# A bidirectional hybrid encoder layer on one Trainium2 core: which queue begins the decay rows' loads

## Chip, cores, metric

One Trainium2 chip, one of its NeuronCores. A core has five engines that run on their own and wait for one another through semaphores: TensorE (PE: matmuls, and PEld, its weight loads), VectorE (DVE), ScalarE (ACT), GpSimd (POOL) and SyncE (SP). Transfers between HBM and SBUF are begun by an instruction in the queue of SyncE, ScalarE or GpSimd and are then carried out by 16 DMA engines. Each queue is worked off in order: an instruction that waits for a semaphore holds back everything behind it in that queue.

The metric is the device time of one execution in microseconds, as the median of several runs.

## The reference

One layer, batch 1, 2048 tokens of width 1024. A normed and modulated input is multiplied by one large matrix; its columns feed two branches, neighbourhood attention on a grid of 64 columns and a bidirectional mLSTM with 4 heads of 128. The outputs are concatenated, multiplied by an output matrix and added to the input through a gate.

```python
mod = c_act @ w_ada + b_ada; shift, scale, gate = split(mod, 3)
h = rmsnorm(x, norm_w) * (1 + scale) + shift
proj = h @ w_in + b_in
na_out = neighbourhood_attention(na_q, na_k, na_v, rpb) * silu(na_z)
h_fwd, h_bwd = mlstm_chunkwise(mq, mk, mv, i_f, f_f), flip(mlstm_chunkwise(flip(...)))
ml_out = norm((h_fwd + h_bwd) * sigmoid(ml_o)) * ml_norm_w * silu(ml_z)
x = rmsnorm(x + gate * (concat(na_out, ml_out) @ w_out), final_norm_w)
```

The part that matters here lies in the mLSTM. Inside a chunk, the score of position t against position s is weighted by a decay matrix:

```python
Dlog = where(lower, b[..., :, None] - b[..., None, :] + i_pre[..., None, :], -inf)
S = einsum('bhntd,bhnsd->bhnts', q, k) * exp(Dlog - m_t[..., None])
```

The reference takes chunks of 64; the kernel takes chunks of 128 (CH), of which there are 16 for each head and direction. With g = i - b and m the running maximum that stabilises the exponent, the weight is exp(g[s] - m[t]) under the triangular mask.

## The kernel before

All matrices are float32 and are multiplied in three passes of float32r parts (high x high, high x low, low x high), so each product of a weight block with a token tile is 24 matmuls.

The kernel runs in stages. `phase1` prepares h, then computes the projection block by block, 256 columns each. `tok_blocks` (blocks 2 to 5) has token-major outputs: `vo_group` for the mLSTM's v and output gate (blocks 2 and 3; blocks 0 and 1 were done in `start`), `nav_group` for the attention's v (blocks 4 and 5). A block has 4 groups of 4 token tiles. PE writes a tile into one of four PSUM banks (`pp`), VectorE adds the bias row and writes it into one of two staging tiles (`stvo`, `stv`; L495 and L460), and a store issued by SyncE brings a full staging tile to HBM (`d_ck<-stvo` at L502, `d_vna<-stv` at L464). The store of a group is put into a list by `defer` and written out at the `flush` at the end of the following group; the group after that needs the same staging tile again. `conv_blocks` (blocks 6 to 9) computes the mLSTM's k and q with channel-major outputs (`pc`), which ScalarE takes from PSUM (`u`, L769). Then `phase1b` runs the mLSTM with the remaining projections as filling, and `phase2` the attention and the output projection, the latter in an order written out by hand.

Beside the matmuls of `tok_blocks` runs `self.chain`, a generator of small steps; each token tile advances it by one. It first computes the gates' prefix sums (`gate_chain`), which ends with writing -m for all 128 rows (direction, head, chunk) to HBM as `d_mneg` (L666), and then the decay matrices (`decays`). These are 16 tiles `dec` of 128 x 1024, one for each head and group of four chunks, each with both directions:

- load: two transfers (L698), one for each direction; four rows of `d_mneg`, 512 numbers in all, are read and written into all 128 partitions (256 KB each). There are two buffers (`wgate` and `gacc`), so the load for tile n+2 needs the store of tile n to have landed;
- GpSimd adds the mask (L706);
- ScalarE takes eight exponentials, one for each chunk and direction (L710);
- ScalarE's queue stores the two halves into `d_ck` (L712), where the mLSTM reads them later.

Between these steps `gate_row` sums the gate's weights, with VectorE multiplying loaded tiles `wide` (L397, L404, L406; loaded by SyncE), and SyncE also issues the weight blocks (`raw`, L189), the bias rows (`brow`, L467) and the bias tables (`d_t<-d_e`, L547). ScalarE rounds a weight block to its high part (L191) and GpSimd subtracts for the low part (L192); GpSimd also sets a column of ones in each `stvo` tile (L484). ScalarE applies the sigmoid of the output gate (L499).

Outside `phase2` the order of each engine's queue is made by the framework's scheduler when the program is built: it takes the instructions of the source, with their dependences, and places them, so that a queue need not follow the source's order exactly.

Of the kernel before, what the change touches and what calls it, by code (L numbers as in the profile page):

```python
# [15 lines left out]
P = 128  # L16
# [42 lines left out]
class Kernel:  # L59
# [621 lines left out]
    def decays(self, pool, beside):  # L681

        nc = self.nc
        mask = pool.tile([P, 2, CH], F32, name="mask")
        nc.gpsimd.memset(mask, 0.0)
        nc.gpsimd.affine_select(out=mask[:, 0, :], in_=mask[:, 0, :], pattern=[[1, CH]], compare_op=ALU.is_ge, fill=-BIG, base=0, channel_multiplier=-1)
        nc.gpsimd.affine_select(out=mask[:, 1, :], in_=mask[:, 1, :], pattern=[[-1, CH]], compare_op=ALU.is_ge, fill=-BIG, base=0, channel_multiplier=1)
        groups = [(h, gi) for h in range(MH) for gi in range(NG)]
        tiles = {}

        def load(n):
            h, gi = groups[n]
            flat = pool.tile([P, D], F32, tag=("wgate", "gacc")[n % 2], bufs=1, name=f"dec_{h}_{gi}")
            t = flat.rearrange("p (d c t) -> p d c t", d=2, c=4)
            for d in range(2):
                r = d * 64 + h * NC + 4 * gi
                src = self.d_mneg[r : r + 4].rearrange("r t -> (r t)").unsqueeze(0)
                nc.sync.dma_start(flat[:, d * 512 : (d + 1) * 512], src.broadcast_to([P, 512]))  # L698
            tiles[n] = t

        load(0)
        load(1)
        yield
        for n, (h, gi) in enumerate(groups):
            t = tiles.pop(n)
            nc.gpsimd.tensor_tensor(t, t, mask.unsqueeze(2).broadcast_to([P, 2, 4, CH]), ALU.add)  # L706
            for d in range(2):
                for o in range(4):
                    c = 4 * gi + o
                    nc.scalar.activation(t[:, d, o, :], t[:, d, o, :], AF.Exp, bias=self.cols["g"][:, d, h, c : c + 1])  # L710
                dst = self.d_ck[h, 4 * gi : 4 * gi + 4, :, 641 + d * CH : 641 + (d + 1) * CH].rearrange("c p t -> p c t")
                nc.scalar.dma_start(dst, t[:, d])  # L712
            yield
            next(beside, None)
            yield
            if n + 2 < len(groups):
                load(n + 2)
            yield
        for _ in beside:
            pass  # L720
# [905 lines left out]
```

## Time and profile before

| | us |
|---|---|
| median of 3 runs | 1402.96 (1400.93 to 1407.99) |
| span of the profiled execution | 1394.1 |
| PE busy in the span | 1312.1 |
| ScalarE, VectorE, GpSimd busy | 527.9, 828.9, 294.3 |

The page of the profiled execution gives its span, from the first to the last instruction; what lies around it in a run's time is not shown by itself. A row of the waits reads: engine and line, what it waited for, us in total, number of times, longest. A row of the timeline reads: start in us, duration, engine, line, operation, out<-in, count, and in brackets the idle time before it with what ended it. "SPq" is SyncE's queue, "ACTq" and "POOLq" those of ScalarE and GpSimd; L numbers are lines of the kernel. Neighbouring instructions of the same line are merged (x4), and the duration then covers all of them with the gaps between.

What the DMA queues carried over the whole run (packets, MB, share of 16 engines' span; q1 is begun by SyncE, q10 by ScalarE, q0 by GpSimd):

```
q1 hardware_dynamic: 178062, 186.45, 49.8%
q0 software_dynamic: 21504, 37.73, 11.1%
q10 hardware_dynamic: 70024, 38.02, 9.6%
```

GpSimd begins no transfer before the mLSTM is over: its first one in the trace of before starts at 998.5 us.

### The profile page before, as it was taken

What the parts mean: (1) busy time and instruction counts of PE and PEld (TensorE: products, weight loads), DVE (VectorE), ACT (ScalarE), POOL (GpSimd) and SP (SyncE); (2) the same over time, 40 slices, a digit from 0 to 9 for tenths busy, and PEclk for the clock granted to TensorE, in tenths of its full rate; (3) what the DMA queues carried; (4) which work ended last, traced back from release to release, by engine and by line L of the source; (5) the groups of instructions that cost most, each with busy time, mean ns of one, the idle gap of its engine ahead of it and who ended that gap; (6) DMA issues with size and microseconds to landing.
All of it is one profiled execution on the core that took longest, in us unless ns stands there. A gap on an engine that the chain in (4) does not pass through costs nothing.

```text
span 1394.1 us, 23365 instructions
## 1 busy us (share of the span) xinstructions
PE 1312.1 (94%) x8052; PEld 1124.8 (81%) x8052; DVE 828.9 (59%) x2563; ACT 527.9 (38%) x1129; POOL 294.3 (21%) x321
## 2 busy tenths in 40 slices
PE   2989999898999999999999998999998999999996
PEld 2989998898877787788878877788886888888885
DVE  6583323111355569146767877877646787777674
ACT  4642335423232323113323322333335555555551
POOL 4453212424101010001213002212312211112111
PEclk9999999999999999999999999999999999999998
DMA  9799438677558675554676787856597897876862
GB/s 325 218 288 222 121 100 236 176 197 193 142 111 213 146 188 159 170 160 140 190 212 200 235 236 216 223 144 182 170 270 220 185 227 166 198 191 168 190 162 74
DMA packets 269707, 263.67 MB, mean 189 GB/s; under 512 B 33466, under 2 KB 230074, under 8 KB 269590
## 3 DMA queue, kind: packets, MB, share of 16 engines
q1 hardware_dynamic: 178062, 186.45, 49.8%
q0 software_dynamic: 21504, 37.73, 11.1%
q10 hardware_dynamic: 70024, 38.02, 9.6%
q8 instruction: 64, 1.05, 0.3%
q14 instruction: 53, 0.43, 0.1%
HBM read 177.57 MB, written 92.72 MB: 194 GB/s over the span
## 4 chain that ended last, share of the span: by engine, by line
PE 53%; DMA 6%; DVE 3%; issue 2%; ACT 1%; POOL 1%; POOLq 0%; SPq 0%; ACTq 0%; DVEq 0%
PE pq L861 21%; PE y L1416 11%; PE pO L1379 4%; PE pT L1364 4%; DMA kv<-d_ck 2%; PE pi L1089 2%; PE pc L425 2%; PE pc L426 2%; PE pc L427 2%; PE px L1087 2%; PE pS L1336 1%; PE pS L1337 1%; PE dc L1035 1%; DMA tab<-d_t 1%; PE a L1074 1%
## 5 line engine op out<-in xcount | busy, mean ns | idle before, releaser
L861 PE MATMUL pq<-hhi,whi_a 128*128 128x512 f32 x512 | 210.7, 412 | 0.8 <-ACT u L769 0.8
L861 PE MATMUL pq<-hlo,whi_a 128*128 128x512 f32 x512 | 210.5, 411 | 0.0
L861 PE MATMUL pq<-hhi,wlo_a 128*128 128x512 f32 x512 | 210.4, 411 | 0.0
L1343 ACT ACTIVATE pbuf<-pbuf,mn 128x480 f32<-128x480 f32 (+5 forms) x128 | 76.4, 597 | 105.3 <-DVE mn L1342 105.3
L861 PEld LDWEIGHTS pq<-hhi,whi_a 128*128 128x128 f32 x512 | 97.6, 191 | 19.2 <-ACT u L769 1.2
L861 PEld LDWEIGHTS pq<-hhi,wlo_a 128*128 128x128 f32 x512 | 97.6, 191 | 18.0
L861 PEld LDWEIGHTS pq<-hlo,whi_a 128*128 128x128 f32 x512 | 97.6, 191 | 17.9
L1416 PE MATMUL y<-hhi,whi_a 128*128 128x512 f32 x256 | 86.0, 405 | 3.4 <-ACT hhi L1317 2.8
L1416 PE MATMUL y<-hhi,wlo_a 128*128 128x512 f32 x256 | 84.3, 399 | 0.0
L835 POOL TENSOR_TENSOR wlo_a<-rawq,whi_a 128x1024 fp32r<-128x1024 f32 x20 | 48.3, 2414 | 166.2 <-ACT whi_a L834 126.9
L1111 POOL TENSOR_TENSOR hm<-hm,ck 128x128 f32<-128x128 f32 x64 | 26.5, 414 | 264.8 <-DVE hm L1110 178.8
L1342 DVE CUSTOM_DVE_ANT_0 pbuf<-pS,tab 128x480 f32<-128x480 f32 (+5 forms) x128 | 64.8, 540 | 28.3 <-PE pS L1337 21.3
L425 PE MATMUL pvo<-whi_b,hhi 128*128 128x256 f32 x256 | 74.7, 292 | 7.1 <-DVE stvo L495 7.1
L1092 ACT ACTIVATE num<-px,gtile 128x129 f32<-128x129 f32 x120 | 38.3, 365 | 97.4 <-PE px L1087 77.4
L1019 DVE TENSOR_SCALAR wv<-kv,gtile 128x129 f32<-128x129 f32 x120 | 36.9, 314 | 63.9 <-PE dc L1035 32.2
L427 PE MATMUL pvo<-whi_b,hlo 128*128 128x256 f32 x256 | 73.5, 287 | 0.0
L426 PE MATMUL pvo<-wlo_b,hhi 128*128 128x256 f32 x256 | 73.5, 287 | 0.0
L710 ACT ACTIVATE dec<-dec,gtile 128x128 f32<-128x128 f32 x128 | 42.0, 392 | 71.6 <-POOL dec L706 60.8
L495 DVE TENSOR_TENSOR stvo<-pvo,brow 128x256 f32<-128x256 f32 x64 | 26.4, 419 | 71.2 <-PE pvo L427 54.9
L460 DVE TENSOR_TENSOR stv<-pv,brow 128x256 f32<-128x256 f32 x32 | 12.4, 420 | 87.9 <-DMA d_vna<-stv 48.4
L1379 PE MATMUL pO<-pt,v 128*64 128x128 f32 (+3 forms) x832 | 61.3, 282 | 0.3 <-ACT pt L1366 0.3
L1364 PE MATMUL pT<-ident,pbuf 128*128 128x128 f32 (+2 forms) x416 | 59.1, 280 | 0.0
(298 smaller groups left out, 3575.2 us busy)
## 6 DMA issues: line engine op xcount, KB each, us to landing
ck<-d_ck SPq DMA_DIRECT2D x64, 384.5 KB
kv<-d_ck SPq DMA_DIRECT2D x120, 128.5 KB
rawq<-in_w_main_dram SPq DMA_DIRECT2D x28, 512.0 KB
raw<-in_w_main_dram SPq DMA_DIRECT2D x20, 512.0 KB
d_ck<-stvo SPq DMA_DIRECT2D x16, 514.0 KB
x<-in_x_dram SPq DMA_DIRECT2D x16, 512.0 KB
wada<-in_w_ada_dram SPq DMA_DIRECT2D x32, 256.0 KB
dec<-d_mneg SPq DMA_DIRECT2D x32, 256.0 KB
```

The source lines that it names most:

```text
L425: nc.tensor.matmul(ps, lhi(k), rhi(k), start=(k == 0), stop=False)
L426: nc.tensor.matmul(ps, lhi(k), rlo(k), start=False, stop=False)
L427: nc.tensor.matmul(ps, llo(k), rhi(k), start=False, stop=(k == KT - 1))
L710: nc.scalar.activation(t[:, d, o, :], t[:, d, o, :], AF.Exp, bias=self.cols["g"][:, d, h, c : c + 1])
L835: nc.gpsimd.tensor_tensor(lo[:, :, cs], raw, hi[:, :, cs].bitcast(F32), ALU.subtract)
L861: nc.tensor.matmul(patch_ps(ps) if patch else ps, w, self.htok(h, g, k, patch), start=(k == 0 and n == 0), stop=(k == KT - 1 and n == 2))
L1092: nc.scalar.activation(num[:, d, :], px[:, d, :], AF.Copy, scale=self.cols["inter"][:, d, h, c : c + 1])
L1342: nc.vector.tensor_tensor_reduce(pt[:, :nk], ps, tabs[place[u]][j][:, :nk], 1.0, 3e38, ALU.add, ALU.min, mn)
L1343: nc.scalar.activation(pt[:, :nk], pt[:, :nk], AF.Exp, bias=mn, scale=-1.0, accum_out=sums[:, j : j + 1])
L1364: nc.tensor.transpose(ps[:cs, i, :], pts[j][:, i * cs : (i + 1) * cs], self.ident)
L1379: nc.tensor.matmul(po[j * HD : (j + 1) * HD, :], v[:n, h * HD : (h + 1) * HD], pt[j][:n, i, :], start=(i == 0), stop=(i == nch - 1))
L1416: nc.tensor.matmul(y, m[:, k, :], w[k][:, cs], start=(k == 4 and n == 0), stop=(k == 3 and n == 2))
```

## The change

The two loads of a `dec` tile are begun by GpSimd's queue. Source, destination, size, number and place in the source stay as they are, and so do all other transfers.

```diff
@@ in decays(), load(n)
             for d in range(2):
                 r = d * 64 + h * NC + 4 * gi
                 src = self.d_mneg[r : r + 4].rearrange("r t -> (r t)").unsqueeze(0)
-                nc.sync.dma_start(flat[:, d * 512 : (d + 1) * 512], src.broadcast_to([P, 512]))
+                nc.gpsimd.dma_start(flat[:, d * 512 : (d + 1) * 512], src.broadcast_to([P, 512]))
             tiles[n] = t
```

## The prediction

> **What bounds the kernel now.** I read the waits of the whole run first, to see which engine sets the end. TensorE is busy 94% of the span, so only a stretch in which it stands still can pay for anything.
>
> ```profile
> PE 1312.1 (94%) x8052; PEld 1124.8 (81%) x8052; DVE 828.9 (59%) x2563; ACT 527.9 (38%) x1129; POOL 294.3 (21%) x321
> ```
>
> The 32 loads are issued between 195.8 and 340 us, in the token-major blocks. The windows table of that stage (PE busy, PEld, DVE, ACT, POOL, then granted clock, DMA share, GB/s) and the waits of PE in it:
>
> ```profile
> 190.00:230.00 40.00, 40.00 (x340) 40.00 (x339) 11.98 (x20) 17.87 (x31) 12.51 (x7) 1.00 0.72 190
> 230.00:270.00 40.00, 32.90 (x261) 32.28 (x260) 11.84 (x17) 17.22 (x38) 9.72 (x6) 0.96 0.72 195
> 270.00:310.00 40.00, 39.11 (x324) 37.90 (x323) 5.73 (x14) 14.33 (x35) 12.47 (x6) 1.00 0.77 189
> 310.00:345.00 35.00, 32.12 (x264) 30.91 (x262) 3.60 (x9) 12.37 (x34) 15.10 (x7) 1.00 0.75 180
> 345.00:360.00 15.00, 11.98 (x87) 11.98 (x88) 2.69 (x7) 5.37 (x17) 3.33 (x2) 0.78 0.88 244
> ...
> PE pvo L425 <- DVE stvo L495: 7.1, 3, 3.7
> PE pv L425 <- DVE stv L460: 6.8, 2, 5.9
> ```
>
> PE idles 7.1 + 0.9 + 2.9 + 3.0 = 13.9 us here, which is the 7.1 + 6.8 of the two waits: always for VectorE to empty a PSUM bank. Behind each idle stretch the granted clock falls as well. Five-microsecond windows:
>
> ```profile
> 250.00:255.00 5.00, 3.32 (x18) 3.32 (x19) 2.62 (x5) 4.10 (x10) 0.32 (x2) 0.76 0.55 158
> ...
> 345.00:350.00 5.00, 1.98 (x9) 1.98 (x10) 1.42 (x4) 3.78 (x12) 3.33 (x2) 0.50 0.98 334
> 350.00:355.00 5.00, 5.00 (x38) 5.00 (x38) 0.42 (x1) 1.44 (x5) 0.00 (x0) 0.85 1.10 246
> ```
>
> Busy time by missing clock: 3.32 x 0.24 = 0.8 us after the earlier stops, 1.98 x 0.50 + 5 x 0.15 = 1.7 us after the last. So 13.9 + 2.5 = 16.4 us (1.2%) is the most that any change to this stage can win.
>
> Why is VectorE late? Its own wait rows, and what SyncE's queue waited for in the same stage:
>
> ```profile
> DVE stv L460 <- DMA d_vna<-stv: 48.4, 5, 16.1
> DVE gsum L406 <- DMA wide<-in_w_ada_dram: 24.0, 6, 10.2
> ...
> SPq L698 <- DMA d_ck<-dec: 65.7, 18, 9.0
> ```
>
> VectorE waits for stores and loads that SyncE issues, and SyncE stands 65.7 us in front of the decay loads (L698), each of which may only start when the store of the tile that held its buffer has landed. SyncE takes its instructions in order, so a store whose data is ready waits there too. The worst case, in SyncE's and VectorE's timelines:
>
> ```profile
> 326.05 0.24 SPq L417 DMA_DIRECT2D d_gate<-wide  x1
> 335.92 4.91 SPq L698 DMA_DIRECT2D dec<-d_mneg  x4
> 340.93 0.38 SPq L464 DMA_DIRECT2D d_vna<-stv  x1
> ...
> 319.38 0.42 DVE L460 TENSOR_TENSOR stv<-pv,brow 128x256 f32<-128x256 f32 x1 [2.42 <-PE pv L427]
> ...
> 347.54 1.42 DVE L460 TENSOR_TENSOR stv<-pv,brow 128x256 f32<-128x256 f32 x4 [16.14 <-DMA d_vna<-stv]
> ```
>
> The staging tile was full at 319.8; its store went out at 340.93, behind four decay loads, and VectorE got the tile back at 347.5. That is PE's 5.9 us stop.
>
> **The change, part by part.** Removed from SyncE: 32 issues and their waits. Added to GpSimd: the same 32 issues and waits, ahead of or between the mask additions (L706), the weight splits (L192) and the memsets (L484). Bytes and destinations stay.
>
> *The last stop.* With L698 gone, the store follows the 326.05 issue and can start about 14.6 us earlier (340.93 against 326.3), and VectorE with it, at 333. PE runs ahead of VectorE by four PSUM banks; a tile is 24 matmuls of 40/340 us, 2.8 us, so the lead is 11.3 us and 14.6 us removes the 5.9 us stop. With its clock: **-7.6 us**. Bounds: 0 (another transfer holds the store) to -7.6.
>
> *The stop of 0.9 us at 293.* The same pattern, with the pair of loads and then the store:
>
> ```profile
> 286.47 0.81 SPq L698 DMA_DIRECT2D dec<-d_mneg  x2
> 287.38 0.38 SPq L464 DMA_DIRECT2D d_vna<-stv  x1
> ```
>
> PE missed 0.9 us in this window, as much as the pair's issue alone kept the store back (286.47 to 287.38). Without it: **-0.9 us**, bounds 0 and -0.9.
>
> *The three stops between 230 and 251 us (7.1 us, 0.8 of clock)* hang on the gate row's weight loads:
>
> ```profile
> 223.08 1.52 SPq L698 DMA_DIRECT2D dec<-d_mneg  x2
> 226.32 0.33 SPq L397 DMA_DIRECT2D wide<-in_w_ada_dram  x1
> ...
> 240.73 1.61 SPq L698 DMA_DIRECT2D dec<-d_mneg  x2
> 242.44 0.37 SPq L397 DMA_DIRECT2D wide<-in_w_ada_dram  x1
> ```
>
> Without the decay loads the 226.32 load could go where they began, at 223.1 (3.2 us earlier), and the 242.44 one about 1.5 us earlier. But the same DMA engines still carry the same bytes (share 0.72), so a load that starts earlier need not land as much earlier. Bounds 0 and -7.9; I take half of the first shift, **-1.6 us**, because the rest depends on landing times.
>
> *The issues on GpSimd.* Its own DMA issues in the later stage, and what they took to land:
>
> ```profile
> L1272 POOL DMA_DIRECT2D v<-d_vna x40: 623/679/807, 1005.5 to 1334.7; - x40
> ...
> v<-d_vna POOLq DMA_DIRECT2D x16, 256.0 KB, 9.4
> wlo_a<-d_mix POOLq DMA_DIRECT2D x8, 256.0 KB, 4.1
> ```
>
> 32 x 0.68 = 22 us more on an engine that is busy 12.5 of 40 us here; hidden under its idle time. What counts is the loop that two buffers make: add, exponentials, store landing, load landing, next add.
>
> ```profile
> 203.08 2.40 POOL L706 TENSOR_TENSOR dec<-dec,mask 128x1024 f32<-128x1024 f32 x1 [3.60 <-DMA dec<-d_mneg]
> ...
> 343.64 2.34 POOL L706 TENSOR_TENSOR dec<-dec,mask 128x1024 f32<-128x1024 f32 x1 [11.28 <-DMA dec<-d_mneg]
> 346.37 2.35 POOL L706 TENSOR_TENSOR dec<-dec,mask 128x1024 f32<-128x1024 f32 x1 [0.39 <-DMA d_vna<-stv]
> ...
> 351.62 0.37 ACTq L712 DMA_DIRECT2D d_ck<-dec  x1
> ```
>
> From SyncE, issue to add took 7.7 us (335.92 to 343.64); from GpSimd an issue lands in 4.1 to 9.4 us. Per pair of tiles the loop changes by -3.6 to +1.7 us, over eight pairs by -29 to +14 us. The chain ends at 351.6 now, and then between 323 and 365. The cover behind it:
>
> ```profile
> 361.27 0.42 DVE L460 TENSOR_TENSOR stv<-pv,brow 128x256 f32<-128x256 f32 x1 [2.42 <-PE pv L427]
> ...
> 360.00:400.00 40.00, 40.00 (x186) 32.77 (x185) 14.83 (x35) 11.15 (x15) 4.84 (x2) 1.00 0.28 84
> ```
>
> PE ends these blocks at 361.3 and has four conv tiles of 24 x 40/186 = 5.2 us before it needs ScalarE, which stands behind the last exponentials: 382, or about 372 when PE arrives 10 us earlier. A chain that ends up to 20 us later costs nothing, so I take **0** for both ends; without the cover each microsecond of delay would cost one.
>
> *ScalarE's lag in the earlier blocks.* The sigmoid (L499) stands among the exponentials, its store releases a staging tile:
>
> ```profile
> 278.44 1.08 DVE L460 TENSOR_TENSOR stv<-pv,brow 128x256 f32<-128x256 f32 x3 [7.50 <-DMA d_ck<-stvo]
> ```
>
> The 7.5 us wait is within PE's 11.3 us lead; 3.8 us are left. Later decay loads here would eat them. Bounds 0 and +4; I take **+1.5 us**.
>
> *Weight splits and memsets behind a waiting load.*
>
> ```profile
> 327.61 2.40 POOL L192 TENSOR_TENSOR wlo_a<-raw,whi_a 128x1024 fp32r<-128x1024 f32 x1
> ```
>
> The last split for the block that begins at 361.3 is done at 330.0, so 31 us of delay are covered; the memsets' column is read only by the store. **0**; a delay past 31 us would stop PE for the excess.
>
> The sum: -7.6 - 0.9 - 1.6 + 1.5 = **-8.6 us**. Span 1394.1 - 8.6 = 1385.5. The page gives the profiled execution's span only; the median of the runs is 1402.96, 8.9 above it, which I carry over: **1394.4 us**.
>
> A rule speaks against this. The Trainium skill, "DMA: Bandwidth & Descriptors", section "Issuing engines are not separate DMA queues", says that transfers begun by different engines run on the same DMA engines and that spreading them saves only the issuing sequencer's time. The rows agree on the engines, but what SyncE loses at L698 is 65.7 us of waiting, not issuing, and that is what is moved; by the rule alone the time would stay near 1403, close to the second rival below.
>
> **The rivals.**
>
> *GpSimd blocks itself; slower.* If a load for tile n+2 stands in GpSimd's queue ahead of the addition for n+1, each tile takes addition, exponentials, store landing and issue in a row, with no overlap of two. Rows: the addition 2.4; 8 x 0.33 = 2.6 for the exponentials (three in 0.99, below); the landing up to what SyncE waited at most, 9.0; two issues 1.4. That is up to 15.4 us a tile against (346.37 - 203.08)/15 = 9.6 now. It decides from 11.0 us a tile on: 203.1 + 15 x 11.0 + 5 (346.37 to the store at 351.62) = 373, where the cover ends. At 12.3 the chain ends at 392.6, PE stops some 20 us at the start of the conv blocks, and with the 8.6 won the time is 1394 + 20 = 1414. For it: the source writes the load before that addition. Against it: ScalarE's queue.
>
> ```profile
> 329.41 0.99 ACT L710 ACTIVATE dec<-dec,gtile 128x128 f32<-128x128 f32 x3 [0.15 <-issue]
> 332.39 0.40 ACT L710 ACTIVATE dec<-dec,gtile 128x128 f32<-128x128 f32 x1 [1.99 <-POOL dec L706]
> 332.40 0.37 ACTq L712 DMA_DIRECT2D d_ck<-dec  x1
> ```
>
> The second store of one tile stands behind an exponential of the next, which waits for that tile's addition; an addition behind a load that waits for this store would lock the queues. So the queues do not follow the source, and with ScalarE's order kept the addition comes first.
>
> *Another wait in the old one's place.* The staging store is earlier, but the gate row's loads or the chain's end take the gain back: the 7.6 falls to 2 or 3, the rest to 0, and 1400 to 1403 results (1402). For it: a DMA share of 0.72 to 0.88 and VectorE's 24.0 us for the weight loads; against it: 14.6 us of freed time before a stop of 5.9.
>
> *It does not do what it says.* SyncE's order is made anew when a queue changes, and its stores may again stand behind waits of other loads; the time is then 1403. No row of the trace shows that order, so the chance is small and not nothing.
>
> **How the numbers follow.** Forecast 0.46 (1394.4, its own range 1387 to 1398); another wait 0.20; no effect 0.07; GpSimd blocks itself, 0.27 with the late chain's smaller losses (1405 to 1420). 0.5% is 7 us, about what a measurement here can tell from no change. Faster than 1396: most of the forecast, 0.43, and little else; slower than 1410: 0.25; between: 0.32. The range runs from 1386 (all of the 16.4 would be 1386.6) to 1414, where one case's upper part is left out.
>
> **What would show it.** Right: no wait of SyncE at L698; d_vna stores issued within a few microseconds of the last addition into their tile; PE's 6.8 us wait on L460 near zero; granted clock 1.00 from 340 to 360; the last stv addition near 352. In GpSimd's timeline two mask additions still come close together and the last before 350. Wrong: mask additions 11 us or more apart, a stop of PE just after the conv blocks begin, or VectorE still waiting over 11 us for d_vna.

## The result, and the profile after

| | before | after |
|---|---|---|
| median, us | 1397.77 (1389.19 to 1407.99) | 1429.19 (1424.00 to 1433.65) |
| span of the profiled execution | 1394.1 | 1426.0 |
| TensorE busy | 1312.1 | 1319.0 |

Six runs of each; the ratio is 1.0235, with a 95% interval of 1.0208 to 1.0261. The change costs 31 us. The prediction, 1394.4 with a range of 1386 to 1414, had the sign wrong, and the time lies above the range.

The windows of the changed kernel, with the columns as before:

```profile
190.00:230.00 40.00, 40.00 (x339) 39.82 (x338) 11.37 (x21) 13.97 (x25) 13.47 (x10) 1.00 0.72 188
230.00:270.00 40.00, 32.23 (x247) 31.82 (x246) 7.04 (x12) 18.58 (x40) 11.15 (x13) 0.87 0.77 166
270.00:310.00 40.00, 28.70 (x211) 28.50 (x212) 4.54 (x12) 14.28 (x30) 15.05 (x11) 0.87 0.68 170
310.00:345.00 35.00, 30.91 (x233) 28.74 (x232) 4.10 (x10) 10.12 (x32) 13.79 (x12) 0.95 0.52 131
345.00:360.00 15.00, 5.27 (x45) 5.06 (x43) 0.00 (x0) 2.68 (x9) 4.60 (x4) 0.76 0.72 145
360.00:400.00 40.00, 29.22 (x197) 28.83 (x198) 4.55 (x13) 8.88 (x20) 10.40 (x7) 0.75 0.49 138
```

From 190 to 400 us PE is busy 166.3 us; before it was 196.1 (the five rows of the prediction and the full 40.00 of the last). The granted clock falls behind the stops as it did before. The same columns from 190 us to the end of PE's last token-major tile, before and then after:

```profile
190.00:361.20 171.20, 157.30 (x1278) 154.28 (x1277) 35.84 (x67) 68.07 (x153) 53.34 (x27) 0.97 0.75 192
190.00:399.20 209.20, 165.54 (x1261) 162.14 (x1260) 31.17 (x67) 67.72 (x154) 67.67 (x55) 0.88 0.65 159
```

The blocks end 38.0 us later. PE idles 43.7 us in place of 13.9, which is 29.8 us more, and is busy 8.2 us longer at a granted clock of 0.88 in place of 0.97. At the end of the span 31.9 us are left; why some 6 us come back in the stages behind is not shown. So the loss lies in the token-major blocks and not in the stages after them. Who stops PE and VectorE there, and what SyncE waits for, in the waits of 190 to 410 us:

```profile
DVE stv L460 <- DMA d_vna<-stv: 75.8, 5, 24.2
PE pv L425 <- DVE stv L460: 36.4, 5, 13.7
...
PE pvo L425 <- DVE stvo L495: 7.3, 1, 7.3
...
SPq L502 <- ACT stvo L499: 53.8, 4, 17.6
SPq L547 <- DMA d_ck<-dec: 39.8, 6, 9.7
SPq L464 <- DMA d_ck<-dec: 21.5, 2, 13.2
SPq L189 <- POOL wlo_a L192: 17.8, 3, 15.2
```

PE's wait for the attention-value staging (L460) grew from 6.8 to 36.4 us, VectorE's wait for the d_vna stores from 48.4 to 75.8. The 65.7 us at L698 are gone from SyncE, but SyncE now waits 132.9 us in the four rows shown, at other places, and all four wait for the decay chain: for the sigmoid, which stands behind the exponentials in ScalarE's queue; for stores of decay tiles; and for a weight split, which stands behind the additions in GpSimd's queue. Neither the table copies (L547) nor the d_vna stores (L464) use the decay tiles' data. In the built program the transfers of SyncE and of ScalarE use eight completion semaphores in turn, and a transfer waits until the previous user of its semaphore has landed; that is often a decay store. The copy that went out at 342.71, shown below, waited for the decay store begun at 335.48.

PE's 43.7 us are six stops. One of 7.3 us at 234 hangs on the gate row's loads, as three of together 7.1 us did before. Two, of 7.4 us at 269.5 and 4.4 us at 290.5, have no counterpart before. The first of them in ScalarE's, SyncE's and VectorE's timelines:

```profile
267.91 0.64 ACT L499 ACTIVATE stvo<-stvo 128x512 f32<-128x512 f32 x1
```

```profile
268.62 0.39 SPq L502 DMA_DIRECT2D d_ck<-stvo  x1
```

```profile
276.43 1.42 DVE L460 TENSOR_TENSOR stv<-pv,brow 128x256 f32<-128x256 f32 x4 [17.76 <-DMA d_ck<-stvo]
```

The sigmoid stood behind the exponentials of a decay tile, the store behind the sigmoid, and VectorE waited for the staging tile. The second has the same order, with the sigmoid at 288.90, the store at 289.61 and VectorE at 294.38 (the profile names a weight split as the last releaser there, which the addition does not read). The last three stops, 4.1 us at 320.5, 13.7 us at 350.3 and 6.8 us at 378.3, hang on d_vna stores: 24.6 us, where there were 0.9 + 5.9 = 6.8 us before.

The last two of these in SyncE's, VectorE's, ScalarE's and GpSimd's timelines:

```profile
342.71 9.37 SPq L547 DMA_DIRECT2D d_t<-d_e  x2
360.45 0.37 SPq L464 DMA_DIRECT2D d_vna<-stv  x1
376.09 2.70 SPq L189 DMA_DIRECT2D raw<-in_w_main_dram  x2
...
380.04 0.39 SPq L464 DMA_DIRECT2D d_vna<-stv  x1
```

```profile
338.92 0.42 DVE L460 TENSOR_TENSOR stv<-pv,brow 128x256 f32<-128x256 f32 x1 [0.36 <-PE pv L427]
363.51 1.42 DVE L460 TENSOR_TENSOR stv<-pv,brow 128x256 f32<-128x256 f32 x4 [24.17 <-DMA d_vna<-stv]
384.63 1.42 DVE L460 TENSOR_TENSOR stv<-pv,brow 128x256 f32<-128x256 f32 x4 [19.70 <-DMA d_vna<-stv]
```

```profile
372.52 2.01 ACT L191 ACTIVATE whi_a<-raw 128x1024 fp32r<-128x1024 f32 x2 [0.15 <-ACT dec L710]
```

```profile
368.40 2.36 POOL L706 TENSOR_TENSOR dec<-dec,mask 128x1024 f32<-128x1024 f32 x1 [5.50 <-DMA dec<-d_mneg]
373.66 4.76 POOL L192 TENSOR_TENSOR wlo_a<-raw,whi_a 128x1024 fp32r<-128x1024 f32 x2 [2.90 <-ACT whi_a L191]
```

A staging tile was full at 339.3 (338.92 + 0.42) and its store went out at 360.45; VectorE stood still for 24.2 us. The next store went out at 380.04, behind weight loads that waited for the split at 373.66; the split waited for the rounding at 372.52, and that stood among the exponentials of the last tile. VectorE lost 19.7 us more.

A stretch of GpSimd's own timeline, with loads that wait for a buffer:

```profile
245.87 1.09 POOL L698 DMA_DIRECT2D dec<-d_mneg  x2 [8.07 <-DMA d_ck<-dec]
253.38 2.38 POOL L706 TENSOR_TENSOR dec<-dec,mask 128x1024 f32<-128x1024 f32 x1 [6.42 <-DMA dec<-d_mneg]
255.70 1.09 POOL L698 DMA_DIRECT2D dec<-d_mneg  x2
260.87 2.39 POOL L706 TENSOR_TENSOR dec<-dec,mask 128x1024 f32<-128x1024 f32 x1 [4.08 <-DMA dec<-d_mneg]
```

and its loads among the DMA issues (size, median us from issue to landing):

```profile
dec<-d_mneg POOLq DMA_DIRECT2D x32, 256.0 KB, 5.0
```

Load, addition, load, addition: the load for tile n+1 stands behind the addition of tile n, which waits for its own load, so after the first pair no two tiles' loads overlap. Before, the later loads went out four transfers in a row (335.92 in the prediction), so the loads of two tiles were under way together, and the two additions came close together (343.64 and 346.37). The additions run from 193.25 to 368.40, (368.40 - 193.25)/15 = 11.7 us a tile, against 9.6 before. A load itself is quick: 1.09 us for the two issues and a median of 5.0 us to land.

### The profile page after: what moved, and what is told of

Read it like the earlier page. It is cut to its first block, busy times and chain, and to the rows that moved or that the text cites. A ratio compares the mean times of both kernels' runs of the same rounds, so it can differ in the third digit from the quotient of the medians.

```text
span 1426.0 us, 23361 instructions
## 1 busy us (share of the span) xinstructions
PE 1319.0 (92%) x8052; PEld 1132.1 (79%) x8052; DVE 823.9 (58%) x2563; ACT 527.7 (37%) x1129; POOL 309.2 (22%) x353
## 3 DMA queue, kind: packets, MB, share of 16 engines
q0 software_dynamic: 24064, 46.12, 13.8%
## 4 chain that ended last, share of the span: by engine, by line
PE 51%; DMA 6%; DVE 3%; issue 2%; ACT 1%; POOL 1%; SPq 0%; POOLq 0%; ACTq 0%; DVEq 0%
PE pq L861 20%; PE y L1416 10%; PE pO L1379 4%; PE pT L1364 4%; DMA kv<-d_ck 3%; PE pi L1089 2%; PE px L1087 2%; PE pc L427 2%; PE pc L426 2%; PE pc L425 2%; PE pS L1336 1%; PE pS L1337 1%; PE dc L1035 1%; DMA tab<-d_t 1%; PE a L1074 1%
## 5 line engine op out<-in xcount | busy, mean ns | idle before, releaser
L861 PEld LDWEIGHTS pq<-hlo,whi_a 128*128 128x128 f32 x512 | 97.4, 190 | 17.8
L460 DVE TENSOR_TENSOR stv<-pv,brow 128x256 f32<-128x256 f32 x32 | 12.2, 419 | 127.8 <-DMA d_vna<-stv 75.8
L425 PE MATMUL pv<-whi_b,hhi 128*128 128x256 f32 x128 | 39.6, 310 | 24.6 <-DVE stv L460 24.6
```

Of the source, the lines that this page charges most:

```text
L425: nc.tensor.matmul(ps, lhi(k), rhi(k), start=(k == 0), stop=False)
L861: nc.tensor.matmul(patch_ps(ps) if patch else ps, w, self.htok(h, g, k, patch), start=(k == 0 and n == 0), stop=(k == KT - 1 and n == 2))
```

## The experiments

Two theories from this reading: Q, that the alternation in GpSimd's queue makes the chain late and that this sets the time; and rivals named with each run. Q fell in the second group, and a theory P took its place. In the diffs, what is written under `issue_after(x)` is placed behind x in its queue. In each group the ratio is taken against runs of the kernel before on the same chip (medians there: 1398.3, 1387.8, 1397.5 and 1388.1 us). The numbers of all kernels stand in one table behind the third group.

### First group: the order of the loads, the table copies, half of the loads

```diff
@@ e1_pairs: even tile's addition queued behind the next tile's loads
-            nc.gpsimd.tensor_tensor(t, t, mask..., ALU.add)
+            with self.tc.issue_after(last[n + 1].ins) if n % 2 == 0 else ExitStack():
+                nc.gpsimd.tensor_tensor(t, t, mask..., ALU.add)
@@ e2_hold: table copies queued behind the newest d_vna store; e3_pairs_hold: both
-                    self.tables_rows(i, rt)
+                    with self.tc.issue_after(self.vna.ins):
+                        self.tables_rows(i, rt)
@@ e4_half: direction 0 by GpSimd, direction 1 by SyncE
-                nc.gpsimd.dma_start(flat[...], src...)
+                (nc.gpsimd if d == 0 else nc.sync).dma_start(flat[...], src...)
```

> The changed kernel, with the mask addition of every even decay tile queued behind the loads of the following odd one, so that GpSimd's queue goes load, load, addition, addition and no load stands behind an addition that waits for another load. Theory Q (the loads stand behind GpSimd's own additions, the decay chain slows from 9.6 to 10.9 us a tile and everything tied to it follows): pace at most 9.5 us a tile, last addition before 350 us, PE's wait for the stv additions under 12 us, time 1388 to 1402. Theory S (the 32 transfers left the rotation of completion semaphores that SyncE and ScalarE share, so SyncE's copies and stores now wait for the decay stores): SyncE still waits over 40 us for d_ck<-dec at the table copies and staging stores, time 1412 or more.

Measured: 1400.25 us, ratio 1.0022 (1.0002 to 1.0042). An edit of GpSimd's order takes the loss away, with every load still begun by GpSimd. But the reason given did not hold: the additions are still 10.9 us apart (191.72 to 355.57), the last one is past 350, and PE's wait of 13.8 us is above 12. The waits of this kernel:

```profile
PE pv L425 <- DVE stv L460: 13.8, 4, 7.5
...
SPq L547 <- DMA d_ck<-dec: 39.7, 8, 12.5
SPq L502 <- ACT stvo L499: 39.0, 4, 14.3
```

SyncE still waits 112.2 us for the chain at the four places (132.9 in the changed kernel), and PE idles only 19.4 us. That was the first sign that neither SyncE's waiting nor the chain's speed decides by itself.

> The changed kernel, with the bias table copies (d_t<-d_e) queued in SyncE behind the last staging store, GpSimd's order as changed. Theory S: the staging stores are no longer held back behind copies that wait for decay stores; PE's wait for the stv additions falls from 36 to under 15 us, time 1395 to 1408. Theory Q: the decay chain keeps 10.5 us a tile or more, ScalarE's sigmoids and the weight splits stay late behind it, time 1415 or more.

Measured: 1429.16, ratio 1.0233 (1.0191 to 1.0276). With the copies out of the way the d_vna stores themselves wait 51.7 us for decay stores (three times, 24.3 at the longest). The copies are not the cause. The additions are 10.7 us apart, less than in e1, and the loss is the full one.

> Both edits of the two runs before. If Q and S each carry a part, this gives the gain that the prediction had for a freed SyncE: 1383 to 1398, PE idle under 8 us between 190 and 362 us. If one of them carries all, it equals the better of the two within 0.5%.

Measured: 1403.12, ratio 1.0050 (1.0025 to 1.0075): as e1, with nothing gained from the held copies.

> Only direction 0 of each decay tile is loaded by GpSimd, direction 1 by SyncE as before. Theory Q: GpSimd's load of the next tile still stands behind an addition in most places and that addition now also waits for SyncE's half; pace 10.3 us a tile or more, time 1415 to 1432. Theory S: half of the transfers are back in SyncE's rotation, about half of the loss, 1405 to 1416.

Measured: 1400.46, ratio 1.0021 (0.9995 to 1.0047). Q's figure is missed, but the run tells little: the scheduler ordered GpSimd's queue in another way, with loads and additions in pairs from the eighth tile on, and SyncE still stood 82.8 us at L698.

### Second group: the weight splits, and the alternation without GpSimd

```diff
@@ e5_dvesplit (e6_dvesplit_hold: with the table copies held; e8_before_dvesplit: in the kernel before)
-            nc.gpsimd.tensor_tensor(lo[:, ks, :256], raw, hi[...], ALU.subtract)
+            (nc.gpsimd if blk < 4 else nc.vector).tensor_tensor(lo[:, ks, :256], raw, hi[...], ALU.subtract)
@@ e7_conv: kernel before, load n+1 made to wait for addition n
-                nc.sync.dma_start(flat[...], src...)
+                ld = nc.sync.dma_start(flat[...], src...)
+                if n > 1:
+                    self.tc.add_manual_dep(ld.ins, adds[n - 1].name, mybir.DependencyInfo(mybir.DependencyClass.Sync, ...))
...
-            if n + 2 < len(groups):
-                load(n + 2)
+            if 0 < n < len(groups) - 1:
+                load(n + 1)
```

> The changed kernel, but from the fifth weight block on VectorE subtracts for a block's low part (L192), so no split stands in GpSimd's queue behind the additions and loads. The order load, addition, load, addition stays. Theory Q (the alternation makes the chain late, and the lateness reaches PE through several of SyncE's waits on it): the additions stay at 11 us a tile or more and SyncE's two waits for stores of decay tiles stay, so most of the loss stays: 1418 to 1432; only SyncE's wait for GpSimd at L189 (17.8 us) disappears, and with it at most the last stop at 378 to 385. Rival W (the splits that now stand behind waiting loads carry the loss): 1398 to 1408.

Measured: 1429.23, ratio 1.0301 (1.0275 to 1.0328). GpSimd's splits do not carry the loss. The stop came back in another form; VectorE's and ScalarE's timelines, and PE's wait:

```profile
355.77 1.23 DVE L192 TENSOR_TENSOR wlo_a<-raw,whi_a 128x1024 fp32r<-128x1024 f32 x1 [42.78 <-ACT whi_a L191]
```

```profile
354.68 1.06 ACT L191 ACTIVATE whi_a<-raw 128x1024 fp32r<-128x1024 f32 x1 [0.15 <-ACT dec L710]
```

```profile
PE pv L425 <- DVE stv L460: 38.2, 2, 32.4
```

VectorE's split for the first conv block waits 42.8 us for ScalarE's rounding, which stands behind the exponentials, and PE stops for 32.4 us in one piece.

> The same, and the three table copies (L547) queued on SyncE behind the last attention-value store. Theory Q: two of the three couplings are cut, and what is left are a staging store's own wait for a decay tile's store and the sigmoid behind the exponentials; PE's wait on L460 falls below 20 us (36.4 in the changed kernel) and the time lies between 1402 and 1418. If either of the two couplings were enough by itself, the time would stay near 1429, as it did with the table copies alone. Rival W: no different from the kernel without the held copies.

Measured: 1439.47, ratio 1.0348 (1.0313 to 1.0384). Q's range is missed on the far side: with two couplings cut the loss is no smaller than in e5. PE's wait on L460 is 29.8 us in one stop, and 16.2 more stand at L499, the staging of the output gate's block in that kernel's line numbers.

> The kernel before, with SyncE's loads, where the load of tile n+1 is now made to wait for the addition of tile n, and is written behind it: the changed kernel's order of additions and loads without any transfer begun by GpSimd. Theory Q: additions 11 us or more apart, the last after 365, and the time goes up to 1415 or more, so the queue that begins the transfer does not matter, only the lost overlap does. Rival S (begun by GpSimd a load is itself slower, or GpSimd's work for beginning it is): additions stay under 10.5 us apart and the time within 0.5% of 1398.

Measured: 1396.13, ratio 1.0058 (1.0038 to 1.0077). The additions are (355.69 - 197.86)/15 = 10.5 us apart, nearly as slow as in e2, e5 and e6, and only 8 us are lost, with SyncE itself blocked 11.6 us more by the new wait. Q falls: a chain of 10.5 to 10.7 us a tile costs 8 us here and 33 to 48 there (2.33% of 1398 to 3.48% of 1388).

> The kernel before with the splits on VectorE from the fifth block on: the control for the two above. VectorE is 59% busy, so both theories expect 1395 to 1403; if it is slower than 1405, the splits on VectorE cost something by themselves and the two readings above must be taken against this.

Measured: 1390.88, ratio 1.0020 (0.9998 to 1.0042). The same splits on VectorE cost nothing in the kernel before; its row beside the 42.8 us of e5:

```profile
DVE wlo_a L192 <- ACT whi_a L191: 14.3, 2, 12.3
```

What differs between e5 and e8 is who begins the loads, and what the scheduler made of it. That led to counting where the rounding stands.

### Third group: the place of the chain in the queues

In ScalarE's queue of the kernel before, the rounding for the first conv block (L191, block 6) stands behind the exponentials of 12.0 of the 16 tiles. In the changed kernel it stands behind 15.6 (it begins at 372.52, shown above), and block 5's behind 7.5 and not 6.1. The row of before:

```profile
317.92 2.01 ACT L191 ACTIVATE whi_a<-raw 128x1024 fp32r<-128x1024 f32 x2 [0.44 <-ACT dec L710]
```

The diff says nothing of ScalarE; the scheduler moved the chain ahead of its neighbours when the loads changed queue. Theory P: the loss comes from that place. The work that PE needs stands behind more tiles of a chain that in the run is later than in the plan.

```diff
@@ e9_anchor (e11_before_anchor: in the kernel before; e12_pairs_anchor: with e1's order)
-            nc.scalar.activation(hi[:, ks, :256], raw, AF.Copy)
-            nc.gpsimd.tensor_tensor(lo[:, ks, :256], raw, hi[...], ALU.subtract)
+            self.hi_i = nc.scalar.activation(hi[:, ks, :256], raw, AF.Copy)
+            self.lo_i = nc.gpsimd.tensor_tensor(lo[:, ks, :256], raw, hi[...], ALU.subtract)
...
+            with self.tc.issue_after(self.lo_i.ins):
                 nc.gpsimd.tensor_tensor(t, t, mask..., ALU.add)
...
+                    with self.tc.issue_after(self.hi_i.ins):
                         nc.scalar.activation(t[:, d, o, :], ..., AF.Exp, ...)
@@ e10_before_ahead: kernel before, block 6's rounding and split issued at the last tile
+                if n == 15:
+                    with self.tc.issue_after(add.ins), self.tc.issue_after(ex.ins):
+                        self.later.pop(0)()
```

> The changed kernel, with one thing more: the additions and exponentials of a tile are queued behind the weight rounding (L191) and the weight split (L192) that stand before them in the source. GpSimd's order load, addition, load, addition stays. In the kernel before, the rounding for the first conv block stands behind the exponentials of 12 tiles on ScalarE's queue, in the changed kernel behind 15.6; here behind 10. Theory P (the loss comes from where the planned order puts the chain: the work behind it waits for a chain that runs later than planned): the additions stay 10.5 us or more apart and the time falls to 1408 or less (before: 1388 to 1398). Theory Q (the lost overlap of the loads sets the time, wherever the rest stands): 1418 or more, as with every earlier kernel that kept the alternation on GpSimd.

Measured: 1397.59, ratio 0.9997 (0.9973 to 1.0022). The whole loss is gone. The chain is no faster than in e2 (the additions from 206.33 to 366.75, 10.7 us a tile) and the last addition is 12 us later than e2's. GpSimd still alternates, except that the two loads before each of the held splits now stand together. Its waits:

```profile
SPq L547 <- DMA d_ck<-dec: 52.3, 11, 14.0
SPq L464 <- DMA d_ck<-dec: 35.1, 4, 14.1
SPq L502 <- ACT stvo L499: 30.0, 5, 19.3
...
DVE stv L460 <- DMA d_vna<-stv: 11.8, 1, 11.8
...
PE kt L817 <- DMA raw<-in_w_main_dram: 8.7, 1, 8.7
PE pvo L425 <- DVE stvo L495: 7.9, 1, 7.9
```

SyncE waits for decay stores even longer than in the changed kernel (52.3 + 35.1 against 39.8 + 21.5 us), but for earlier ones, and so in time. The second to fifth d_vna stores go out at 280.8, 303.3, 313.4 and 322.2 us, when ScalarE has issued the stores of 7, 9, 10 and 10 tiles; in the changed kernel at 320.9, 333.0, 360.5 and 380.0, after 10, 11, 14 and 16 tiles. VectorE's wait for them falls from 75.8 to 11.8 us, and of PE's wait on L460 1.5 us is left, at the first conv tile. What is left is the 8.7 us stop after the conv blocks have begun, which the profile puts down to a weight load: the chain's last store is issued at 371.9 there, close to the 373 that the first rival gave as the end of the cover.

> The kernel before, with SyncE's loads; only the rounding and the split of the first conv block's weights are queued behind the last tile's exponentials and addition (15.5 and 16 tiles, as in the changed kernel, and not 12). No transfer moves and the pace of the chain stays at 9.6 us a tile. Theory P, if this one place is enough without the slower chain: SyncE's next weight loads wait for the split until about 355 us and PE stops in the first conv block or just before it, 5 to 25 us more than before. If place and pace are both needed: within 0.5% of before, since the chain ends at 351 to 355 and PE needs the weights at 361. Theory Q: no change.

Measured: 1390.19, ratio 0.9938 (0.9909 to 0.9966). None of the numbers expected: not slower, but faster. The place of this one rounding and split is harmless; PE's wait on L460 is 1.0 us and not 6.8. Why it is faster is not shown. GpSimd has no split between its late additions there (324.56 and 327.34, where the kernel before has 325.27, a split, and 329.96).

> The kernel before with the same edit as the first of these (rounding and split behind 10 tiles and not 12): shows what the edit does by itself. Both theories: within 0.5% of before, 1385 to 1400; if P is right, none slower, since the chain's neighbours wait less.

Measured: 1388.14, ratio 0.9941 (0.9914 to 0.9967): better than the lower side of "within 0.5%", and faster than both kernels. Block 6's rounding stands behind 10 tiles and PE no longer waits on L460 at all. Its two rows from 310 to 360 us, where the kernel before lost its 5.9 us stop:

```profile
310.00:345.00 35.00, 35.00 (x289) 34.00 (x289) 5.35 (x12) 10.25 (x32) 9.97 (x5) 1.00 0.78 191
345.00:360.00 15.00, 15.00 (x93) 13.37 (x92) 2.58 (x8) 7.82 (x19) 8.31 (x4) 1.00 0.69 197
```

> Both mended: loads begun by GpSimd in pairs (load, load, addition, addition) and the rounding and split queued ahead of the chain. Theory P: no worse than the pairs alone (ratio 1.002), and if SyncE's freed queue is worth what the prediction said (up to 8.6 us), a ratio of 0.994 to 1.000. If the ratio stays at 1.002 or above, SyncE's freed time is worth nothing because its stores wait for other transfers instead.

Measured: 1391.68, ratio 0.9952 (0.9928 to 0.9976). Inside P's range, and no better than e11, which leaves the loads with SyncE. What is gained comes from the order of the queues, though not from the place of the chain alone, since e10 gained as much with one rounding and split put behind it. Moving the loads adds nothing that these runs can show.

### Fourth group: the place alone

```diff
@@ e13_before_early3: kernel before, in vo_group where h == 3 and in nav_group (e14_before_early2: in vo_group alone)
             next(self.chain, None)
+            next(self.chain, None)
```

> The kernel before, with SyncE's loads; the chain is advanced by two steps and not one for each token tile of blocks 3 to 5, so that the planned order puts it further ahead: block 5's weight rounding behind 8 tiles (before 6.1, changed 7.5), the first conv block's behind 15 (before 12, changed 15.6). No transfer moves and loads keep their pairs. Theory P with the place alone: the same neighbours wait, and the time goes up by 10 us or more (ratio 1.007 or more). Place and pace both needed (P2): the chain still takes 9.6 us a tile or less, and the ratio stays under 1.005. Theory Q also expects under 1.005.

Measured: 1404.75 (1394.56 to 1409.30), ratio 1.0120 (1.0063 to 1.0177), as P by itself expected and not P2 or Q. The profiled execution is the quickest of the four, and even it shows the pattern; first and last addition and PE's wait:

```profile
198.25 2.40 POOL L709 TENSOR_TENSOR dec<-dec,mask 128x1024 f32<-128x1024 f32 x1 [3.34 <-DMA dec<-d_mneg]
...
341.57 2.39 POOL L709 TENSOR_TENSOR dec<-dec,mask 128x1024 f32<-128x1024 f32 x1 [3.32 <-issue]
```

```profile
PE pv L425 <- DVE stv L460: 19.2, 3, 11.0
```

The pace is 9.6 us a tile as before, no transfer is moved, and PE's wait on L460 grows from 6.8 to 19.2 us. So the place costs by itself, here about half of what the change costs. That the rest takes the slower chain as well is not shown: the place here is 15.0 tiles and not 15.6.

> The same with two steps in block 3 only: 8 and 14 tiles. By P alone about half of the first one's loss, and by P2 and Q again under 1.005.

Measured: 1386.07, ratio 0.9991 (0.9969 to 1.0014). Not half of the loss but none, as P2 and Q expected: 14 tiles at (334.75 - 200.47)/15 = 9.0 us a tile are still in time.

All kernels together: the tiles whose exponentials stand ahead of block 6's rounding in ScalarE's queue as built, the distance of the additions in the trace, PE's wait on L460, and the ratio. In e10 only that rounding and split were moved; wherever else the place differs from 12.0, the chain moved as a whole.

| kernel | loads by | tiles ahead | us a tile | PE on L460, us | ratio |
|---|---|---|---|---|---|
| before | SyncE | 12.0 | 9.6 | 6.8 | 1 |
| e8 | SyncE | 12.0 | 9.5 | 2.0 | 1.0020 |
| e7 | SyncE | 12.0 | 10.5 | 10.1 | 1.0058 |
| e11 | SyncE | 10.0 | 9.4 | none | 0.9941 |
| e14 | SyncE | 14.0 | 9.0 | 6.7 | 0.9991 |
| e13 | SyncE | 15.0 | 9.6 | 19.2 | 1.0120 |
| e10 | SyncE | 15.5 (one block) | 9.5 | 1.0 | 0.9938 |
| e4 | both | 13.6 | 9.8 | 9.2 | 1.0021 |
| e9 | GpSimd | 10.0 | 10.7 | 1.5 | 0.9997 |
| e12 | GpSimd | 10.0 | 10.4 | none | 0.9952 |
| e1 | GpSimd | 13.4 | 10.9 | 13.8 | 1.0022 |
| e3 | GpSimd | 13.4 | 10.7 | 10.3 | 1.0050 |
| after | GpSimd | 15.6 | 11.7 | 36.4 | 1.0235 |
| e2 | GpSimd | 15.8 | 10.7 | 32.6 | 1.0233 |
| e5 | GpSimd | 15.6 | 10.6 | 38.2 | 1.0301 |
| e6 | GpSimd | 16.0 | 10.6 | 29.8 | 1.0348 |

Read it by the columns. At 10.4 to 10.9 us a tile the ratio runs from 0.9952 to 1.0348 and follows the place: nothing is lost at 10, up to 0.6% at 12 to 13.4, 2.3 to 3.5% from 15.6 on. At SyncE's pace of 9.0 to 9.6 us nothing is lost up to 14, and 1.2% at 15; e10, with one block's rounding moved, loses nothing at 15.5.

## Why the prediction was wrong

The terms of the sum against PE's idle time, after less before, in the stops named above:

| term | predicted, us | idle time, us |
|---|---|---|
| the last stop and the one at 293 (d_vna stores) | -7.6 and -0.9 | 24.6 - 6.8 = +17.8 |
| the stops between 230 and 251 (gate row) | -1.6 | 7.3 - 7.1 = +0.2 |
| ScalarE's lag (sigmoid) | +1.5 | +11.8 |

*The last stop, -7.6.* This step failed first and cost most. It said that with L698 gone "the store follows the 326.05 issue", as if the rest of the queues' order stayed. The waits at L698 did vanish. But SyncE's, ScalarE's and GpSimd's orders were all made anew, and the store inherited waits for the same chain at other places (132.9 us). The stop did not vanish; in its place stand three, 24.6 us of PE's time, the last two with 24.2 and 19.7 us of waiting on VectorE. The 0.9 and the 1.6 us rested on the same premise and went with it; the gate row's load of 226.32 went out at 232.55, and VectorE waited 32.4 us at L406 in place of 24.0.

```profile
DVE gsum L406 <- DMA wide<-in_w_ada_dram: 32.4, 4, 13.8
```

*The issues on GpSimd, 0.* The price of an issue was about right (1.09 us for two, 5.0 us to land, within 4.1 to 9.4). What was missing is the position of the load in GpSimd's queue: behind the addition of the tile before. The chain's end at 375.4 (last store) lies 10 us past the upper bound of 365, although the first addition was 10 us earlier than before.

*ScalarE's lag, +1.5.* The right place and a size far too small. The last two sigmoids stood behind the exponentials of 6.0 and 7.5 tiles and not of 5.0 and 6.4, and SyncE waited 53.8 us for it where it had waited 9.2. PE stopped for 11.8 us behind these two (in e9 both stand behind 5.0, and PE has no such stop); the bound of +4 was taken from the pattern of before, with its order. The row of before:

```profile
SPq L502 <- ACT stvo L499: 9.2, 4, 6.4
```

*Weight splits behind a waiting load, 0.* The 31 us of cover were counted to PE's use of the weights. The split is also waited for by the next weight loads in SyncE's queue, and behind these stood a d_vna store. That wait (15.2 us at the longest) ended in the stop at 378 us, before PE needed any of those weights. By itself it was not decisive: e5 took the split away from GpSimd and the loss stayed.

*The rivals.* "GpSimd blocks itself" had the right sign and the right loss of overlap, but its order is the mirror image of the real one: not load n+2 ahead of addition n+1, but addition n ahead of load n+1. The argument that ScalarE's order forbids the first held (the timeline never shows it), and was then taken as if it left only the harmless order. Its threshold of 11.0 us a tile is not where the loss begins: e2 loses 2.3% at 10.7, where e9 loses nothing. A stop in the first conv block is found in e9 (8.7 us), not in the changed kernel, whose stops lie in blocks 3 to 5. "It does not do what it says" named what happened, SyncE's order made anew with stores behind waits of other loads, and priced it at no change with a chance of 0.07, because no row showed that order. That a row does not show an order is no reason for a small chance.

*The rule that speaks against the change.* By the Trainium skill, "DMA: Bandwidth & Descriptors", section "Issuing engines are not separate DMA queues", beginning transfers on several engines saves only the sequencer's time to begin them. The runs agree that nothing is gained by GpSimd's queue (e12 at 0.9952 beside e11 at 0.9941); the loss of 31 us is outside of what the rule speaks of.

*The 8.9 us carried over.* They were taken as the part of a run that lies around the span. In the runs with both figures that part is 1.7 to 2.5 us (1427.85 against 1426.0 for the profiled run of the changed kernel). So most of the 8.9 was the distance of the median from a quicker profiled run; over all six runs the kernel before has a median of 1397.77. This shifts the forecast by some 7 us and does not explain the miss.

*The signs named beforehand.* Of those for wrong, two came: additions more than 11 us apart (11.7) and VectorE waiting over 11 us for d_vna (24.2). Of those for right, only the first, no wait at L698.

*What is not settled.* Why the scheduler puts the chain ahead when GpSimd begins the loads is open. No run changed the shared completion semaphores by themselves; e9 has the longer waits for them and no loss, so they are not enough. How the loss divides between place and pace is open too: 1.2% for a place of 15.0 at SyncE's pace (e13), 0.6% for a pace of 10.5 at the old place (e7), 2.35% for 15.6 and 11.7 together.

## What to carry to other kernels

When a scheduler orders the queues, an edit of one instruction's engine can be an edit of all queues: compare the built orders of every engine first, and count how many steps of the slow chain stand ahead of each instruction that the busy engine needs. A wait that is removed from an in-order queue is not removed from what stands behind it, if that too depends on the chain; here 65.7 us went and, in the four rows shown, 14.5 us became 132.9. Try holding the side chain behind the main path's preparation (e11) before moving transfers between queues; here that gained 0.6%, about the 8.6 us that the move was meant to gain.

## What was unexpected of the hardware

Putting two loads side by side again (e1) did not make the chain faster: 10.9 us a tile, against 10.7 in e2, where they alternate with the additions. The overlap that the prediction and theory Q counted on was small. GpSimd's timeline of e1:

```profile
254.99 1.09 POOL L698 DMA_DIRECT2D dec<-d_mneg  x2 [3.73 <-DMA d_ck<-dec]
264.91 1.07 POOL L698 DMA_DIRECT2D dec<-d_mneg  x2 [8.83 <-DMA d_ck<-dec]
265.99 2.40 POOL L707 TENSOR_TENSOR dec<-dec,mask 128x1024 f32<-128x1024 f32 x1
```

The second load of a pair still waits for its own buffer, here 8.8 us and 2.2 to 4.3 us in the other pairs, until the store of the tile in it has landed. In this pair the first tile's addition stands behind that wait and then begins at once, 11.0 us after its own load was begun. Landing takes a median of 6.7 us in e1:

```profile
dec<-d_mneg POOLq DMA_DIRECT2D x32, 256.0 KB, 6.7
```

That is more than the 5.0 us of the changed kernel, but it is not what keeps the pace: e3 and e12, with the same pairs, land in 5.2 and 5.3 us and run at 10.7 and 10.4 us a tile.
